# Two-block transformer kernel on one core: zero rows in the latent keys, a written order for the first microseconds, and dilated attention interleaved with the next projections

## The chip, the cores and the metric

The kernel runs on one core of one Trainium2 chip. The metric is the device time of one execution in microseconds (us), taken as the median of the runs.

## The reference

A batch of one with 256 tokens of width 1024 goes through four layers of a first block and one layer of a second block, all in float32. Cut to what matters here:

```python
def mla_attention(x, w_down, q_norm, kv_norm, w_uq, w_ukv, w_o, cos_r, sin_r):   # layer 2 of 4
    ...
    sc = (jnp.einsum('bqhd,bkhd->bhqk', qn_b, k_nope)          # 128 wide, each head its own keys
          + jnp.einsum('bqhd,bkd->bhqk', qr_b, k_rope)) * scale  # 64 wide, one key for all 8 heads
    ...

def swa_sink_attention(x, w_qkv, sinks, w_o, cos, sin):        # layers 0 and 3
    qkv = x @ w_qkv
    ...

def dilated_attention(q, k, v, pos):                           # second block
    # 24 heads of 64 = 3 groups (window 128, 512, 2048; dilation 1, 4, 16) x 8 slots;
    # softmax over the keys of all three groups of a slot, partial rotary on q and k
    ...

def second_block(x, ...):
    proj = rmsnorm(h) @ w_in
    rq, rk, rv, rg, aq, ak, av, gr, ga = jnp.split(proj, ...)
    yr = retention(rq, rk, rv, positions)    # 4 heads
    ya = dilated_attention(aq, ak, av, positions)
    ...
```

## The kernel before

**Arithmetic.** Every projection is done in three passes of a reduced float32 type: each weight and each activation is split into a high part (ACT, line 200) and a low part (DVE, line 201), and TensorE multiplies high by high, high by low and low by high (lines 214 to 216 and 222 to 224, or two wider passes at 248 and 252). The attention products (lines 702, 739, 968, 969, 992, 993, 1234, 1273) use plain float32, and the trace shows two TensorE records for each of them. Transposes go through TensorE with an identity (line 279).

**Data flow.** Weights come from HBM on one queue (SP, line 101) in pieces of 512 KB into five buffers `raw`, and are split into nine pairs of buffers `wh`, `wl`. `Cols.load` issues the DMA and `Cols.get` splits. PSUM has eight banks: `acc` 2, `sc` 2, `tr` 2, `po` 1, `tq` 1. The activation `x` lies as two tiles of 128 tokens, `xT` is its transposed, split form.

**Order.** The program is written as one stream; a scheduler of the tile framework then sets the order on each engine from its own estimate, so that an instruction can pass others on its engine. `Skew.unit` (line 140) runs attention in three steps: the scores and the softmax of a unit, then the transposes of the unit before it (`turn`), then the values of the one before that; `Skew.step` (line 145) takes after these `pieces` steps of a generator `fill`, if one is set. `defer` puts a transpose off until a given number of projection columns has been issued.

**The start.** `setup` (line 379) loads `x[0]` in two halves, two weight pieces of layer 0's key and value projection, `x[1]`, and the other two weight pieces; `x_xT(0)` transposes and splits `x[0]`. `swa` (line 652) then projects keys and values of token tile 0 (`kv(0)`), transposes `x[1]`, does `kv(1)`, the queries, and fills its attention units with `memkv` (line 409): the memory inputs `mem` are loaded into the four buffers `e` and transposed, and projected by `mem_w_kv`.

**Layer 2, latent attention** (`mla`, line 901). `krT` holds the 64-wide rotary key of all heads, transposed, twice: in rows 0 to 63 and 64 to 127. `qrT` holds the rotary queries of two heads in each 128 rows. `scores` (line 963) adds, for each token tile, a product over 128 rows (line 968) and one over 64 rows (line 969), in the upper or lower half of rows by the parity of the head.

**Dilated attention** (`mixer2`, line 1362). For each of four pairs of slots, `dil_proj` (phase dp0 to dp3) projects keys, queries and values of both token tiles (six projections of 24 matmuls) and `dil_attn` (phase da0 to da3) runs two units, one for each token tile. The scores of tile 0 take three groups in two banks `sc`; those of tile 1 take two groups in `sc` and the third in the two banks `acc`, which the projections use too. Two heads lie in the two halves of the rows. After the four pairs comes retention, its first projection in phase rp0.

## Time and profile before

| what | value |
|---|---|
| median of 3 runs | 2066.47 us (2066.15 to 2066.87) |
| the profiled execution's own time | 2067.32 us |
| its span, first to last instruction | 2065.5 us |
| PE busy | 2027.3 us, 98% |
| DVE, ACT busy | 77%, 60% |
| POOL busy | 39.8 us, 2% |
| mean granted TensorE clock | 0.995 |

PE is TensorE's matmul stream and PEld its weight loads; ACT is ScalarE, DVE VectorE, POOL GpSimd, SP the queue that issues the DMAs. A PE record overlaps the next one, so what a matmul costs is read from start to start, not from its duration. In a list of waits, "A <- B" says that A stood idle until B had finished. The granted clock is a share of 2.4 GHz; 0.5 is the lower level of 1.2 GHz.

### The profile page before, as it was taken

The numbers are of one execution on the slowest core, as the hardware profiler recorded it, in microseconds if no ns is written. First come the engines' busy times: TensorE is split into PE (matmuls) and PEld (weight loads), VectorE is DVE, ScalarE is ACT, GpSimd is POOL, SyncE is SP. The second block draws the span as 40 slices with busy tenths as digits, with TensorE's granted clock in tenths as the row PEclk, the third lists the DMA queues.
The fourth block names the chain that finished last, engine by engine and source line by source line (L and its number), as shares of the span: only waits on it lengthen the run. The fifth ranks groups of instructions, "written<-read, shape, count | busy, mean of one in ns | idle before, by whom it ended". The sixth has DMA issues, their size and how long they took to land.

```text
span 2065.5 us, 30420 instructions
## 1 busy us (share of the span) xinstructions
PE 2027.3 (98%) x10741; PEld 1704.8 (83%) x10741; DVE 1587.2 (77%) x3144; ACT 1247.6 (60%) x2592; POOL 39.8 (2%) x54
## 2 busy tenths in 40 slices
PE   7999999999999999999999999999999999999998
PEld 6878888887888888888887788888898888788887
DVE  7766898899699877779888778988666666576666
ACT  5844666595477645557666557665666554456554
POOL 0000000000000000000000000000000000000000
PEclk9999999999999999999999999999999999999999
DMA  7453666446457543555655435764546556566662
GB/s 267 129 166 122 223 204 194 154 135 235 142 179 225 169 161 119 184 189 161 214 163 161 145 127 203 224 191 119 160 120 202 164 175 200 175 193 208 196 187 79
DMA packets 236649, 359.65 MB, mean 174 GB/s; under 512 B 13904, under 2 KB 157392, under 8 KB 236496
## 3 DMA queue, kind: packets, MB, share of 16 engines
q1 hardware_dynamic: 236496, 357.71, 54.8%
q8 instruction: 84, 1.38, 0.3%
q14 instruction: 69, 0.57, 0.1%
HBM read 356.60 MB, written 1.05 MB: 173 GB/s over the span
## 4 chain that ended last, share of the span: by engine, by line
PE 51%; DVE 3%; ACT 2%; issue 1%; DMA 1%; POOL 0%; SPq 0%; POOLq 0%; DVEq 0%; ACTq 0%
PE b2f.sc L248 2%; PE b2f.tr L248 2%; PE b3f.sc L248 1%; PE b3f.tr L248 1%; PE mlp.sc L248 1%; PE mlp.tr L248 1%; PE mlp.acc L214 1%; PE mlp.acc L216 1%; PE mlp.acc L215 1%; PE b2f.acc L216 1%; PE b2f.sc L252 1%; PE b3f.acc L214 1%; PE b2f.acc L214 1%; PE b3f.acc L216 1%; PE b3f.acc L215 1%; PE b2f.acc L215 1%
## 5 line engine op out<-in xcount | busy, mean ns | idle before, releaser
L201 DVE TENSOR_TENSOR mlp.wl<-mlp.raw,mlp.wh 128x512 fp32r<-128x512 f32 x132 | 86.1, 687 | 41.5 <-ACT mlp.wh L200 40.6
L200 ACT ACTIVATE mlp.wh<-mlp.raw 128x512 fp32r<-128x512 f32 x132 | 75.8, 624 | 38.4 <-PE mlp.tq L216 20.8
L200 ACT ACTIVATE b0f.wh<-b0f.raw 128x512 fp32r<-128x512 f32 x132 | 76.3, 623 | 29.7 <-PE b0xo.tq L216 11.1
L200 ACT ACTIVATE b2f.wh<-b2f.raw 128x512 fp32r<-128x512 f32 x132 | 76.2, 623 | 29.1 <-PE b2xo.tq L216 11.0
L200 ACT ACTIVATE b1f.wh<-b1f.raw 128x512 fp32r<-128x512 f32 x132 | 76.2, 622 | 28.6 <-PE b1xo.tq L216 11.2
L200 ACT ACTIVATE b3f.wh<-b3f.raw 128x512 fp32r<-128x512 f32 x132 | 76.4, 622 | 25.9 <-PE b3xo.tq L216 9.8
L201 DVE TENSOR_TENSOR b0f.wl<-b0f.raw,b0f.wh 128x512 fp32r<-128x512 f32 x132 | 85.6, 684 | 5.2 <-ACT b0f.wh L200 5.0
L201 DVE TENSOR_TENSOR b2f.wl<-b2f.raw,b2f.wh 128x512 fp32r<-128x512 f32 x132 | 85.6, 683 | 4.7 <-ACT b2f.wh L200 4.6
L201 DVE TENSOR_TENSOR b1f.wl<-b1f.raw,b1f.wh 128x512 fp32r<-128x512 f32 x132 | 85.6, 684 | 4.6 <-ACT b1f.wh L200 4.4
L201 DVE TENSOR_TENSOR b3f.wl<-b3f.raw,b3f.wh 128x512 fp32r<-128x512 f32 x132 | 85.7, 683 | 4.2 <-ACT b3f.wh L200 3.9
L248 PE MATMUL b3f.sc<-b3xo.xT,b3f.wh 128*128 128x512 f32 x144 | 52.4, 398 | 1.0 <-DVE b3f.e L545 1.0
L248 PE MATMUL b1f.sc<-b1xo.xT,b1f.wh 128*128 128x512 f32 x144 | 52.4, 398 | 0.0
L248 PE MATMUL b2f.sc<-b2xo.xT,b2f.wh 128*128 128x512 f32 x144 | 52.4, 398 | 0.0
L248 PE MATMUL b0f.sc<-b0xo.xT,b0f.wh 128*128 128x512 f32 x144 | 52.4, 398 | 0.0
L248 PE MATMUL b2f.tr<-b2xo.xT,b2f.wh 128*128 128x512 f32 x144 | 51.8, 395 | 0.0
L248 PE MATMUL b0f.tr<-b0xo.xT,b0f.wh 128*128 128x512 f32 x144 | 51.7, 394 | 0.0
L248 PE MATMUL b1f.tr<-b1xo.xT,b1f.wh 128*128 128x512 f32 x144 | 51.7, 394 | 0.0
L248 PE MATMUL b3f.tr<-b3xo.xT,b3f.wh 128*128 128x512 f32 x144 | 51.7, 394 | 0.0
L545 DVE SCALAR_TENSOR_TENSOR b1f.e<-b1f.p,b1x.cols,b1f.e 128x255 f32<-128x255 f32 (+1 forms) x72 | 34.2, 479 | 6.8 <-ACT b1f.e L543 6.3
L545 DVE SCALAR_TENSOR_TENSOR b2f.e<-b2f.p,b2x.cols,b2f.e 128x255 f32<-128x255 f32 (+1 forms) x72 | 34.2, 478 | 6.8 <-ACT b2f.e L543 6.4
L545 DVE SCALAR_TENSOR_TENSOR b0f.e<-b0f.p,b0x.cols,b0f.e 128x255 f32<-128x255 f32 (+1 forms) x72 | 34.2, 478 | 5.7 <-ACT b0f.e L543 5.3
L545 DVE SCALAR_TENSOR_TENSOR b3f.e<-b3f.p,b3x.cols,b3f.e 128x255 f32<-128x255 f32 (+1 forms) x72 | 34.2, 478 | 5.6 <-ACT b3f.e L543 5.1
(1642 smaller groups left out, 7081.5 us busy)
## 6 DMA issues: line engine op xcount, KB each, us to landing
b0f.raw<-in_f_w_up_dram SPq DMA_DIRECT2D x44, 512.0 KB
b1f.raw<-in_f_w_up_dram SPq DMA_DIRECT2D x44, 512.0 KB
b2f.raw<-in_f_w_up_dram SPq DMA_DIRECT2D x44, 512.0 KB
b3f.raw<-in_f_w_up_dram SPq DMA_DIRECT2D x44, 512.0 KB
mlp.raw<-in_w_up_dram SPq DMA_DIRECT2D x32, 512.0 KB
mlp.raw<-in_w_down_dram SPq DMA_DIRECT2D x32, 512.0 KB
b0f.raw<-in_f_w_down_dram SPq DMA_DIRECT2D x22, 512.0 KB
b1f.raw<-in_f_w_down_dram SPq DMA_DIRECT2D x22, 512.0 KB
```

Of the source, the lines that this page charges most:

```text
L200: self.nc.scalar.activation(hi, src, AF.Copy)
L201: self.nc.vector.tensor_sub(lo, src, hi.bitcast(F32))
L214: mm(ps, Th[:, k, tok(t)], wh, start=start, stop=False)
L215: mm(ps, Th[:, k, tok(t)], wl, start=False, stop=False)
L216: mm(ps, Tl[:, k, tok(t)], wh, start=False, stop=stop)
L248: mm(ps.rearrange("p a n -> p (a n)"), wh[:, cs], self.xT[:, k].rearrange("p a n -> p (a n)"), start=k == 0, stop=k == w.K - 1)
L252: mm(ps[:, 1], wl[:, cs], self.xTh[:, k], start=False, stop=False)
L545: nc.vector.scalar_tensor_tensor(hc[:, j, s:], ps[j][:, : T - s], cc[:, 2 - s, f : f + 1], hc[:, j, s:], ALU.mult, ALU.add)
```

## The change

It has three parts that share no instruction.

1. **Start.** Each engine's order is fixed by hand (TensorE, ACT, DVE) from the first instruction to the end of the key and value projection. TensorE begins with 8 transposes of the identity that nobody reads, then those of `x[0]`, then 10 more idle ones; the projections of the two token tiles run interleaved, the second two weight pieces behind, into `acc` and `po`. The first weight piece comes in two DMAs, `x[1]` in two halves between the weights.
2. **Latent keys.** `krT` gets a copy for each parity of the head, the other 64 rows zero (one memset on POOL, and four copies of 64 rows instead of two of 128 on DVE), and the 64-row product becomes one over 128 rows.
3. **Dilated attention.** `dil_proj` becomes a generator of six pieces; three pieces of the next pair's projections (for the last pair: of retention's first) are taken after each unit's scores. In the scores of tile 1 both banks `sc` and both banks `acc` are read before the maxima are taken.

```diff
+WARM = (8, 10)
...
-        for n in range(2):
-            nc.sync.dma_start(self.x[0][:, col(n)], I["x"][0, tok(0), col(n)])
-        for k in (0, 2):
-            self.first.load(k)
-        nc.sync.dma_start(self.x[1], I["x"][0, tok(1), :])
+        rows(0, 0)
+        rows(0, 1)
+        self.first.load(0, True)
+        rows(1, 0)
+        self.first.load(2)
+        rows(1, 1)
         for k in (4, 6):
             self.first.load(k)
...
+    def warm(self, n):
+        ps = self.ps("sc", (4, P))
+        for j in range(n):
+            self.nc.tensor.transpose(ps[:, j % 4], self.ident, self.ident)
...
+        def kv_first():
+            pss = [self.ps("acc"), self.ps("po")]
+            with self.in_order():
+                self.warm(WARM[0])
+                for n in range(2):
+                    self.x_xT(0, n)
+                self.warm(WARM[1])
+                for s in range(KD + 2):
+                    if s < KD:
+                        self.mm_nat(pss[0], self.xTh, self.xTl, s, 0, wkv.get(s), s == 0, s == KD - 1)
+                    if s in (1, 4):
+                        self.x_xT(1, s // 4)
+                    if s >= 2:
+                        self.mm_nat(pss[1], self.xTh, self.xTl, s - 2, 1, wkv.get(s - 2), s == 2, s == KD + 1)
...
-        krT = mp.tile([P, T], F32, name=self.nm("krT"))
+        krT = mp.tile([P, 2, T], F32, name=self.nm("krT"))
+        nc.gpsimd.memset(krT, 0.0)
...
-                    nc.tensor.matmul(o, qrT[r0 : r0 + 64, t, hl // 2], krT[r0 : r0 + 64, :nk], start=False, stop=True)
+                    nc.tensor.matmul(o, qrT[:, t, hl // 2], krT[:, hl % 2, :nk], start=False, stop=True)
...
-        for sp in range(4):
-            self.phase = f"dp{sp}"
-            pr = self.dil_proj(sp)
+        pr, rp = [], []
+        for _ in self.named("dp0", self.dil_proj(pr, 0)):
+            pass
+        sk.pieces = 3
+        for sp in range(4):
+            nx = rp if sp == 3 else []
+            sk.fill = self.named("rp0", self.ret_proj(nx, 0)) if sp == 3 else self.named(f"dp{sp + 1}", self.dil_proj(nx, sp + 1))
             self.phase = f"da{sp}"
             self.dil_attn(sp, pr, *ya, sk)
-        sk.flush()
+            for _ in sk.fill:
+                pass
+            pr = nx
+        sk.rest()
```

**ACT, the first instructions.** `xT` is the split form of `x`, `raw` and `wh` are the weights of the key and value projection. Before:

```order
L200 ACT_TABLE_LOAD
L200 ACTIVATE b0swa.wh_142<-start.raw_90 128x512 x2
L200 ACTIVATE b0swa.wh_154<-start.raw_92 128x512 x2
L200 ACTIVATE start.xT_99<-start.tr_100 128x4x128
L200 ACTIVATE start.xT_99<-start.tr_107 128x4x128
L200 ACTIVATE b0swa.wh_166<-start.raw_95 128x512 x2
L200 ACTIVATE b0swa.wh_178<-start.raw_97 128x512 x2
```

Now:

```order
L205 ACT_TABLE_LOAD
L205 ACTIVATE start.xT_101<-b0swa.tr_142 128x4x128
L205 ACTIVATE start.xT_101<-b0swa.tr_149 128x4x128
L205 ACTIVATE b0swa.wh_167<-start.raw_90 128x512 x2
L205 ACTIVATE start.xT_101<-b0swa.tr_179 128x4x128
L205 ACTIVATE b0swa.wh_186<-start.raw_94 128x512 x2
L205 ACTIVATE b0swa.wh_204<-start.raw_97 128x512 x2
L205 ACTIVATE start.xT_101<-b0swa.tr_213 128x4x128
```

The split of `x[0]` has moved ahead of the first weights; the first split of `x[1]` stands ahead of the second weight piece.

**SP, the loads around the memory inputs.** `mem` is the memory input, `mem_w_kv` its weights. Before:

```order
L101 DMA b0swa.raw_1020<-in_mem_w_kv_dram 128x4x256
L101 DMA b0swa.raw_1040<-in_mem_w_kv_dram 128x4x256
L101 DMA b0swa.raw_1109<-in_mem_w_kv_dram 128x2x512
L101 DMA b0swa.raw_1123<-in_mem_w_kv_dram 128x2x512
L416 DMA b0swa.e_527<-in_mem_dram 128x512
L416 DMA b0swa.e_536<-in_mem_dram 128x512
```

Now:

```order
L106 DMA b0swa.raw_1045<-in_mem_w_kv_dram 128x4x256
L106 DMA b0swa.raw_1065<-in_mem_w_kv_dram 128x4x256
L434 DMA b0swa.e_552<-in_mem_dram 128x512
L434 DMA b0swa.e_561<-in_mem_dram 128x512
L434 DMA b0swa.e_619<-in_mem_dram 128x512
L434 DMA b0swa.e_628<-in_mem_dram 128x512
L106 DMA b0swa.raw_1134<-in_mem_w_kv_dram 128x2x512
```

The memory inputs have moved ahead of two of the ten weight pieces that were issued before them.

**PE, the first pair of dilated attention.** `da0.sc` and `da0.acc` are scores, `dp1.acc` a projection of the next pair, `da0.tr` the transposes of tile 0's probabilities. Before, the end of tile 0's scores and what follows:

```order
L1234 MATMUL da0.sc_14901<-dp0.B_14558,dp0.C_14559 128x128
L1234 MATMUL da0.sc_14902<-dp0.B_14558,dp0.C_14559 128x128
L1234 MATMUL da0.acc_14936<-dp0.B_14558,dp0.C_14559 128x256
L1234 MATMUL da0.acc_14937<-dp0.B_14558,dp0.C_14559 128x256
L1234 MATMUL da0.sc_14926<-dp0.B_14558,dp0.C_14559 128x256 x2
L1234 MATMUL da0.sc_14927<-dp0.B_14558,dp0.C_14559 128x256 x2
L214 MATMUL dp1.acc_14970<-dp1.wh_14975,b3f.xT_14437 128x384
L215 MATMUL dp1.acc_14970<-dp1.wl_14976,b3f.xT_14437 128x384
L216 MATMUL dp1.acc_14970<-dp1.wh_14975,b3f.xT_14437 128x384
```

Now, the scores of tile 1, which stand 72 projection matmuls and two groups of transposes behind those of tile 0:

```order
L1283 MATMUL da0.sc_15143<-dp0.B_14586,dp0.C_14587 128x256
L1283 MATMUL da0.sc_15144<-dp0.B_14586,dp0.C_14587 128x256
L1283 MATMUL da0.sc_15143<-dp0.B_14586,dp0.C_14587 128x256
L1283 MATMUL da0.sc_15144<-dp0.B_14586,dp0.C_14587 128x256
L1283 MATMUL da0.acc_15151<-dp0.B_14586,dp0.C_14587 128x256
L1283 MATMUL da0.acc_15152<-dp0.B_14586,dp0.C_14587 128x256
L284 MATMUL da0.tr_15173<-ident,da0.p_14923 128x128 x3
L284 MATMUL da0.tr_15179<-ident,da0.p_14924 128x128 x3
L284 MATMUL dp1.tq_15206<-ident,dp1.e_15129 128x128 x3
L219 MATMUL dp1.acc_15184<-dp1.wh_15027,b3f.xT_14465 128x384
L220 MATMUL dp1.acc_15184<-dp1.wl_15028,b3f.xT_14465 128x384
```

The two tiles' scores stood next to each other and now stand apart; the projection that needs a bank `acc` again stands behind nine transposes.

## Rows read from the trace of the kernel before

**Rows 1.** The page, part 1: busy us (share of the span) xinstructions.
```profile
PE 2027.3 (98%) x10741; PEld 1704.8 (83%) x10741; DVE 1587.2 (77%) x3144; ACT 1247.6 (60%) x2592; POOL 39.8 (2%) x54
```
**Rows 2.** Timeline of PE, 0 to 20 us: start, us, engine, instruction [idle before].
```profile
3.91 1.94 PE L279 MATMUL start.tr<-ident,x 128*128 128x128 f32 x8 [3.91 <-DMA x<-in_x_dram]
...
10.32 0.79 PE L214 MATMUL b0swa.acc<-b0swa.wh,start.xT 128*128 128x512 f32 x1 [4.46 <-ACT start.xT L200]
...
14.39 0.63 PE L214 MATMUL b0swa.acc<-b0swa.wh,start.xT 128*128 128x512 f32 x1
14.82 0.51 PE L215 MATMUL b0swa.acc<-b0swa.wl,start.xT 128*128 128x512 f32 x1
15.17 0.39 PE L216 MATMUL b0swa.acc<-b0swa.wh,start.xT 128*128 128x512 f32 x1
...
19.81 0.50 PE L214 MATMUL b0swa.acc<-b0swa.wh,start.xT 128*128 128x512 f32 x1 [0.61 <-ACT start.xT L200]
```
**Rows 3.** Timeline of ACT, 3 to 13 us.
```profile
7.25 1.15 ACT L200 ACTIVATE b0swa.wh<-start.raw 128x512 fp32r<-128x512 f32 x2 [5.24 <-DMA start.raw<-in_a_w_qkv_dram]
...
9.69 1.06 ACT L200 ACTIVATE start.xT<-start.tr 128x512 fp32r<-128x512 f32 x2
```
**Rows 4.** Waits of PE, whole span: us in total, times, longest us.
```profile
PE b0swa.tq L279 <- DMA b0swa.e<-in_mem_dram: 1.6, 1, 1.6
```
**Rows 5.** Timeline of the SP queue, 25 to 60 us.
```profile
25.98 19.35 SPq L101 DMA_DIRECT2D b0swa.raw<-in_mem_w_kv_dram  x10
45.39 3.83 SPq L416 DMA_DIRECT2D b0swa.e<-in_mem_dram  x4
```
**Rows 6.** Stretches: us, PE, PEld, DVE, ACT, POOL busy, granted clock, DMA share, GB/s.
```profile
50.00:55.00 5.00, 3.45 (x16) 2.82 (x17) 2.27 (x7) 3.44 (x14) 0.00 (x0) 0.76 0.50 184
1435.00:1440.00 5.00, 4.98 (x22) 4.90 (x23) 2.36 (x8) 2.63 (x5) 0.00 (x0) 0.66 0.27 80
1460.00:1465.00 5.00, 3.27 (x12) 3.19 (x13) 3.47 (x11) 2.90 (x10) 0.00 (x0) 0.73 0.39 111
```
**Rows 7.** Timeline of PE, layer 2: one head's scores and what follows.
```profile
768.98 0.38 PE L968 MATMUL b2mla.sc<-b2mla.q 128*128 128x128 f32 x2
769.29 0.49 PE L969 MATMUL b2mla.sc<-b2mla.krT,b2mla.qrT 64*128 64x128 f32 x2
...
770.96 0.39 PE L222 MATMUL b2mla.acc<-b2mla.cq,b2mla.wh 128*128 128x256 f32 x1
```
**Rows 8.** Timeline of PE, layer 0's cross attention: float32 scores over 128 rows.
```profile
158.99 1.02 PE L462 MATMUL b0x.sc<-memk,b0x.q 128*128 128x256 f32 x4
159.85 0.64 PE L279 MATMUL b0x.tq<-ident,b0x.e 128*128 128x128 f32 x4
```
**Rows 9.** Line 928: duration ns min/median/max, first and last start us.
```profile
L928 DVE COPY b2mla.krT<-b2mla.tr x2: 282/283/284, 764.6 to 764.8; 128x128 f32<-128x128 f32 x2
```
**Rows 10.** Timeline of PE, 1452 to 1472 us: the first pair of dilated attention.
```profile
1453.90 0.33 PE L215 MATMUL dp0.acc<-dp0.wl,b3f.xT 128*128 128x384 f32 x1
1454.07 0.33 PE L216 MATMUL dp0.acc<-dp0.wh,b3f.xT 128*128 128x384 f32 x1
...
1454.86 0.94 PE L1234 MATMUL da0.sc<-dp0.B,dp0.C 64*128 64x128 f32 x12
1455.63 0.60 PE L1234 MATMUL da0.acc<-dp0.B,dp0.C 64*128 64x256 f32 x4
1457.48 1.59 PE L1234 MATMUL da0.sc<-dp0.B,dp0.C 64*128 64x256 f32 x8 [1.25 <-DVE da0.p L1237]
1461.73 0.41 PE L214 MATMUL dp1.acc<-dp1.wh,b3f.xT 128*128 128x384 f32 x1 [2.66 <-DVE da0.pb L1237]
...
1471.88 0.38 PE L279 MATMUL dp1.tq<-ident,dp1.e 128*128 128x128 f32 x2
```
**Rows 11.** Timeline of DVE, second pair: masking of tile 1's scores in `sc`, then `acc`.
```profile
1495.21 1.29 DVE L1237 SCALAR_TENSOR_TENSOR da1.p<-da1.sc,dmask 128x512 f32<-128x512 f32 x2 [0.37 <-PE da1.sc L1234]
...
1497.99 0.75 DVE L1237 SCALAR_TENSOR_TENSOR da1.pb<-da1.acc,dmask 128x256 f32<-128x256 f32 x2
```

More of the change, by code (lines that the diff above doesn't have):

```diff
@@ L89, in __init__, with load @@
         self.got, self.raws = {}, {}
-    def load(self, k):
+    def load(self, k, apart=False):
         net, ncol = self.net, self.ncol
@@ L99, in load @@
             dst = r[:, : n * ncol]
-            if len(src.shape) == 3:
+            if apart:
+                for i in range(n):
+                    net.nc.sync.dma_start(dst[:, i * ncol : (i + 1) * ncol], src[:, i])
+            elif len(src.shape) == 3:
                 net.nc.sync.dma_start(dst.rearrange("p (a n) -> p a n", a=n), src)
@@ L394, in setup, with rows @@
         self.first = self.cols(I["a_w_qkv"][0], 1024, 512)
-        for n in range(2):
-            nc.sync.dma_start(self.x[0][:, col(n)], I["x"][0, tok(0), col(n)])
-        for k in (0, 2):
-            self.first.load(k)
-        nc.sync.dma_start(self.x[1], I["x"][0, tok(1), :])
+        def rows(t, n):
+            nc.sync.dma_start(self.x[t][:, col(n)], I["x"][0, tok(t), col(n)])
+        rows(0, 0)
[4 more added lines that the diff above has]
+        rows(1, 1)
         for k in (4, 6):
@@ L402, in setup, with in_order, x_xT @@
         self.new_xT()
-        self.x_xT(0)
-    def x_xT(self, t):
-        for n in range(2):
-            self.to_xT(t, n, self.x[t][:, col(n)])
+    def in_order(self):
+        E = mybir.EngineType
+        return self.tc.manual_schedule(engines={E.PE, E.Activation, E.DVE})
+    def warm(self, n):
+        ps = self.ps("sc", (4, P))
+        for j in range(n):
+            self.nc.tensor.transpose(ps[:, j % 4], self.ident, self.ident)
+    def x_xT(self, t, n):
+        self.to_xT(t, n, self.x[t][:, col(n)])
     def memkv(self, mp):
@@ L665, in kv, with kv_heads @@
             self.proj_nat(ps, self.xTh, self.xTl, t, wkv)
+            kv_heads(t, ps)
+        def kv_first():
[12 more added lines that the diff above has]
+                        self.mm_nat(pss[1], self.xTh, self.xTl, s - 2, 1, wkv.get(s - 2), s == 2, s == KD + 1)
+            for t in range(NT):
+                kv_heads(t, pss[t])
+        def kv_heads(t, ps):
             nc.scalar.activation(v[:, t], ps[:, 256:512], AF.Copy)
@@ L753, in swa @@
         out = mo(oTh, oTl)
-        kv(0)
         if j:
+            kv(0)
             kv(1)
@@ L768, in swa @@
         else:
-            self.x_xT(1)
-            kv(1)
+            kv_first()
             qT = q(0, 0)
@@ L927, in norm, with turn @@
             self.rope(pb[:, None, 256:320], 1, t, [kd[:, 0:1], kd[:, 1:2]])
-            self.defer(KRW * 512, None, lambda: nc.vector.tensor_copy(
-                krT[:, tok(t)], self.transp(kd.rearrange("p a d -> p (a d)"), 1)[:, 0]))
+            def turn():
+                pt = self.transp(kd.rearrange("p a d -> p (a d)"), 1)[:, 0]
+                for par in range(2):
+                    r = slice(64 * par, 64 * par + 64)
+                    nc.vector.tensor_copy(krT[r, par, tok(t)], pt[r])
+            self.defer(KRW * 512, None, turn)
         sc = 192.0 ** -0.5
@@ L959, in attn @@
             hl = h % 4
-            r0 = 64 * (hl % 2)
             p = self.s("p", [384])
@@ L1166, in o4, with dil_proj @@
         return [self.op.tile([P, 4, T], F32R, tag=t, name=self.nm(t)) for t in ("oh", "ol")]
-    def dil_proj(self, sp):
+    def dil_proj(self, out, sp):
         nc = self.nc
@@ L1176, in dil_proj @@
         kT, qT, v = self.b2("B", [3, T]), self.b2("C", [3, T]), self.b2("A", [2, 384])
+        out += [qT, kT, v]
         wk, wq, wv = cols(7680), cols(6144), cols(9216)
@@ L1198, in dil_proj @@
             roped(wk, kT, t)
+            yield
             roped(wq, qT, t)
+            yield
         for t in range(NT):
@@ L1203, in dil_proj @@
             nc.scalar.activation(v[:, t], ps, AF.Copy)
-        self.need()
-        return qT, kT, v
+            if t:
+                self.need()
+            yield
     def dil_attn(self, sp, qkv, yh, yl, sk):
@@ L1239, in scores @@
                                                        ALU.mult, ALU.add)
-                    if i == 0:
-                        for h in range(2):
-                            nc.vector.tensor_reduce(mx[:, 0, h : h + 1], sms[h][0].rearrange("p g n -> p (g n)"), AX, ALU.max)
-                    else:
-                        nc.vector.tensor_reduce(mx[:, 1], both, AX, ALU.max)
-                        nc.vector.tensor_tensor(mx[:, 0], mx[:, 0], mx[:, 1], ALU.max)
+                for h in range(2):
+                    nc.vector.tensor_reduce(mx[:, 0, h : h + 1], sms[h][0].rearrange("p g n -> p (g n)"), AX, ALU.max)
+                if t:
+                    nc.vector.tensor_reduce(mx[:, 1], both, AX, ALU.max)
+                    nc.vector.tensor_tensor(mx[:, 0], mx[:, 0], mx[:, 1], ALU.max)
                 nc.vector.tensor_scalar_mul(nm, mx[:, 0], -1.0)
@@ L1380, in ret_out @@
                                 lambda a, n=n: a[:, col(n)])
-        self.phase = "rp0"
-        rp = []
-        for _ in self.ret_proj(rp, 0):
-            pass
         sgr, sga = [], []
```

## The prediction

> **What bounds the kernel now.** I read the page's busy shares first. TensorE (PE) is busy for 98% of the span, and no other engine for more than 77% [rows 1]. A part of the change can gain only in two ways: by removing one of the short stretches in which PE waits or runs at the lower clock, or by making PE's own work shorter. The list of waits and the timelines show where each part of the change touches such a stretch. The reader should look in them at the starts of PE's rows, and at the idle time in brackets.
>
> *Start.* PE transposes `x[0]` from 3.91 us and then stands still until 10.32, 4.46 us of it for the split of `xT` on ACT [rows 2]. ACT has done nothing until the first weights landed at 7.25. It then splits two weight pieces, and `xT` only at 9.69 [rows 3]. From 10.32 the projections run at 1.2 GHz: two starts lie 0.43 us apart at 14.39, and the duration of one falls from 0.63 to 0.39 us at 15.17, so the clock rose to 2.4 GHz shortly before [rows 2]. PE waits once more, 0.61 us, for `x[1]` at 19.81 [rows 2]. PE then waits 1.6 us for the memory inputs [rows 4]. Their DMAs stood at 45.39 behind ten weight loads that took the queue 19.35 us [rows 5]. The granted clock of that stretch is 0.76 [rows 6].
>
> *Latent keys.* One head's scores take PE from 768.98 to 770.96, 1.98 us. The switch to the 64-row form shows in the rows: two passes of 128 columns over 128 rows start 0.31 us before the first 64-row pass [rows 7]. Four float32 passes of 256 columns over 128 rows, in another stage, take 158.99 to 159.85 together, 0.215 us each [rows 8].
>
> *Dilated attention.* In the first pair the two tiles' scores stand next to each other, and nothing but the softmax is there to do. PE waits 1.25 and 2.66 us, and the next stretch of 45 projection matmuls ends only at 1471.88 [rows 10], with a granted clock of 0.73 between 1460 and 1465 [rows 6]. I did not find such holes in the other three pairs.
>
> **The change, part by part.** The sum is made against the profiled execution's 2067.32 us; the median of the runs lies 0.85 us lower.
>
> *1, the start.* The 18 idle transposes need no data and stand in PE's holes. At the lower clock a transpose costs 1.94 / 8 = 0.24 us [rows 2], so 8 take 1.9 us, before the data's 3.91, and 10 take 2.4 us, from 5.8 to some 8.2. With `xT` ahead of the weights on ACT, the first projection waits for the first weights alone: they land no earlier than 7.25, since the same bytes stand ahead of them, and one split takes 1.15 / 2 = 0.58 us [rows 3], hence 7.8; the idle transposes could hold it to 8.2. I take 7.8, since a rising clock shortens them; that is 2.5 us before 10.32. If the clock is up by then, the 4.6 us from 10.32 to 14.9 at half speed [rows 2] no longer cost 2.3. The 0.6 us at 19.81 goes too. That is 5.4. Against it stands a new wait: on ACT the second weight piece is now split behind the first half of `x[1]`, whose transposes follow six projections on PE; 1.06 / 2 + 0.58 = 1.1 us [rows 3], and DVE's low parts run beside it. **4.3 us** remain; bounds 2.0 (the clock stays low as long as today) and 5.4.
>
> The memory inputs move ahead of two of ten weight loads on SP, so 19.35 / 10 = 1.9 us each [rows 5] or some 3.9 us earlier, while PE comes there some 4 us earlier. I take it that the 1.6 us [rows 4] go, since the burst of loads ahead of them is shorter, and the clock with them: 0.76 over 5 us is 2.4 us at half speed, 1.2 us [rows 6]. The two loads that they pass hold weights used late in the stage; if this cover fails, PE pays at most the 1.9 us of one load. **2.8 us**, bounds 0 and 2.8.
>
> *2, the latent keys.* With all passes over 128 rows a head needs four of 256 columns at 0.215 [rows 8] and four of 128; half the columns make an estimate of 0.11. The sum is 1.30 us for 1.98, so 0.68 us for each of 8 heads: **5.4 us**. The matmul after the switch may gain another 0.1 each; that is the upper bound, 6.2. The lower bound is nothing, if the softmax of a head sets the pace. I take 5.4: the PE timeline has no hole there today. DVE gets two more copies of 0.28 us [rows 9], before the heads start, beside PE's projections; without that cover they cost 0.6. The memset on POOL, which is busy for 2% [rows 1], is issued a layer earlier.
>
> *3, dilated attention.* From the first scores to 1471.88 takes 17.02 us. The same instructions without waits: scores of tile 0 up to 1455.63, 0.77; of tile 1 at most 0.60 + 1.59; six transposes at half of 0.24, 0.7; 45 projection matmuls at 1454.07 - 1453.90 = 0.17, 7.8 [rows 2, 10]. That makes 11.5, a gain of 5.5: the two waits (3.9), 1.35 us of clock (0.73 over 5 us [rows 6]) and some switching. What covers the softmax then is 72 projection matmuls, 12 us. Where the cover is thin is behind tile 1's scores: the next projection needs a bank `acc`, which DVE frees after masking the two `sc` tiles (1.29) and the two `acc` tiles (0.75) [rows 11]. DVE can begin once the first scores are done, and PE has the rest of the scores and nine transposes to do meanwhile, so I expect under 0.5 us there. The other three pairs lose a split of tile 1's scores around transposes; no row prices that, bounds 0 and 2, and I take 1.0, nearer to the bound that the smooth rows suggest. **6.5 us**, bounds 4.5 (a new wait of 1 us, nothing from the other pairs) and 7.5. The loads of the decay tables on SP move with the units; they are used once a head of retention.
>
> The Trainium skill, "TensorEngine Tiling (Array Packing)", section "Overview", says that a contraction of 64 or less can run up to twice as fast in tiles of 64 rows, because tiles in different rows work independently. It speaks against filling up with zero rows; by it the latent part would lose instead of gaining. The trace decides: in the dilated scores, where both halves hold a head, 12 passes of 128 columns take 0.77 us, 0.064 each [rows 10]; but a head of the latent layer uses one half only, and its 64-row passes have no partner.
>
> Sum: 4.3 + 2.8 + 5.4 + 6.5 = 19.0 us. 2067.32 - 19.0 = 2048.3, and at the median's level 2066.47 - 19.0 = **2047.5 us**.
>
> **The rivals.** What a measurement can tell from no change is about 0.2%, 4.1 us.
>
> *A, the start gives back.* The idle transposes leave the clock where it is, and the memory inputs, the DMAs being no faster than before, are waited for as today. For it: the eight real transposes at 3.91 were followed by projections at 1.2 GHz [rows 2], though 4.5 idle us lie between. Against it: the second batch closes this gap. It costs 2.3 + 2.8 us: 2052.6. The Trainium skill, "TensorE: Matmul & The Clock Gate", section "Part 4: PE-mode transpose", says that the full clock does not engage for transposes; by that rule this rival's first half holds. No row here decides it. I give it 0.16 as a whole.
>
> *B, the zero rows gain nothing.* If the softmax sets the pace of the heads, 5.4 is missing: 2052.9. If 64-row passes in different halves do overlap, as in the dilated scores, the full rows even cost: two passes at 0.11 - 0.064 and two at 0.215 less 1.59 / 8 = 0.20 [rows 8, 10], 0.12 us a head, 1.0 in all, so 2053.9. Against both stands the 1.98 us itself [rows 7], which passes that overlap or wait for nothing can't explain. Together 0.14. The tiling page named above would have the second.
>
> *C, slower: the units fight for banks.* The projections now stand between all scores and share `acc` (and retention's first ones `sc`) with them. If each of the eight units then stops PE as the first pair does today, 2.66 us [rows 10] and 1.35 us of clock [rows 6], they cost 8 x 4.0 = 32 us: 2047.5 + 32 = 2079.5. It outweighs the gains from 19.0 / 8 = 2.4 us a unit on. For it: DVE works in order, and weight splits can stand ahead of the masking. Against it: in the order for the first pair nine transposes stand between, and the first bank needs 2 us. 0.03.
>
> *D, the change doesn't do what it says.* The scheduler already drew ten projection matmuls into the first pair, and what PE saves early it may wait for later, at DMAs. Then the time stays within 0.2%. Against it: the latent part shortens PE's own work. 0.05.
>
> **How the numbers follow.** The forecast gets 0.62, A 0.16, B 0.14, C 0.03, D 0.05. Faster by over 0.2% are the forecast, A and B: 0.92; the same D: 0.05; slower C: 0.03. The range begins where the upper bounds of the parts (1.1 + 0.8 + 1.0) and one dip of the clock elsewhere that moves away, like that at 1435 (0.66 over 5 us, 1.7 us [rows 6]), add up, 4.6 below: 2042.9. It ends 2 us above B's dearer case, room for half of A on top of it: 2056.0.
>
> **What would show it.** Right: PE's first projection near 7.8 us, with starts 0.22 us apart by 9; no wait on the memory inputs and a clock of 1.00 around 50; 1.3 us for a head's scores in layer 2 and no new idle there; no idle over 0.5 us in phases da0 to da3. Wrong: starts 0.43 us apart until 12 or later (A), PE waiting for the softmax in layer 2 (B), waits of `acc` on DVE behind tile 1's scores (C).

## The result, and the profile after

| | before | after |
|---|---|---|
| median of 4 runs, same chip | 2066.31 us (2065.15 to 2066.87) | 2048.61 us (2047.92 to 2050.74) |
| ratio of the times | | 0.9917, 95% interval 0.9906 to 0.9928 |
| the profiled execution: time, span | 2067.32, 2065.5 us | 2047.92, 2046.1 us |
| PE idle in the span (span less busy) | 38.2 us | 27.2 us |

The medians lie 17.7 us apart; 2047.5 us was predicted. Between the two profiled executions it is 19.4 us of span: the one of after is its fastest of four, and the one of before, taken apart from the four timed runs, is slower than all of them. The lines of the page that answer to [rows 1]:

```profile
PE 2018.9 (99%) x10759; PEld 1701.3 (83%) x10759; DVE 1586.5 (78%) x3146; ACT 1244.9 (61%) x2592; POOL 40.2 (2%) x55
```

PE has 18 instructions more, the idle transposes, and is busy for 8.4 us less. Where the time went is read best from the first PE row of each phase in the two timelines:

| PE reaches | before, us | after, us | earlier by |
|---|---|---|---|
| the first scores of layer 0 | 37.78 | 34.78 | 3.0 |
| phase b0mo (layer 0's output projection) | 122.83 | 117.22 | 5.6 |
| phase b2mla (latent attention) | 737.86 | 732.26 | 5.6 |
| phase b2mo | 807.49 | 796.27 | 11.2 |
| phase b3x (last cross attention) | 1169.38 | 1157.92 | 11.5 |
| phase b3xo | 1208.59 | 1196.06 | 12.5 |
| phase dp0 | 1423.15 | 1410.56 | 12.6 |
| phase da0 (dilated scores) | 1454.86 | 1440.83 | 14.0 |
| phase ra0 (retention) | 1616.86 | 1597.56 | 19.3 |
| phase ple (the end) | 2034.31 | 2015.01 | 19.3 |

Five steps stand out: 3.0 and 2.6 at the start, 5.6 in the latent layer, 1.44 between dp0 and da0, 5.3 in the dilated part; 1.06 comes between b3x and b3xo, and some 0.3 in scattered places. Two of these steps, 1.44 and 1.06, lie where the change does nothing.

**Start.** PE's timeline of after, as in [rows 2]; the first six rows are an answer for 0 to 14 us, the others are from one for 6.5 to 48 us, which cuts the second batch of idle transposes at its last six.

```profile
1.36 1.97 PE L422 MATMUL b0swa.sc<-ident 128*128 128x128 f32 x8 [1.36 <-POOL ident masks.py:199]
3.58 2.02 PE L284 MATMUL b0swa.tr<-ident,x 128*128 128x128 f32 x8 [0.26 <-DMA x<-in_x_dram]
5.40 1.71 PE L422 MATMUL b0swa.sc<-ident 128*128 128x128 f32 x10
6.90 0.50 PE L219 MATMUL b0swa.acc<-b0swa.wh,start.xT 128*128 128x512 f32 x1
7.62 0.50 PE L220 MATMUL b0swa.acc<-b0swa.wl,start.xT 128*128 128x512 f32 x1 [0.23 <-DVE b0swa.wl L206]
...
8.67 0.39 PE L221 MATMUL b0swa.acc<-b0swa.wh,start.xT 128*128 128x512 f32 x1
...
6.25 0.86 PE L422 MATMUL b0swa.sc<-ident 128*128 128x128 f32 x6
...
10.71 0.50 PE L219 MATMUL b0swa.acc<-b0swa.wh,start.xT 128*128 128x512 f32 x1 [1.21 <-ACT b0swa.wh L205]
11.51 0.50 PE L220 MATMUL b0swa.acc<-b0swa.wl,start.xT 128*128 128x512 f32 x1 [0.30 <-DVE b0swa.wl L206]
...
25.39 0.66 PE L284 MATMUL b0swa.tq<-ident,b0swa.q 128*128 128x128 f32 x4 [0.40 <-ACT b0swa.kT L709]
...
34.78 1.16 PE L741 MATMUL b0swa.sc<-b0swa.kT,b0swa.q 64*128 64x128 f32 x16 [0.31 <-ACT b0swa.q L716]
```

From start to start the first four idle transposes of the second batch take (6.25 - 5.40) / 4 = 0.21 us each, the last six (6.90 - 6.25) / 6 = 0.11. So the clock rose from 1.2 to 2.4 GHz at about 6.3 us, and PE had executed nothing but transposes until then. The first projection comes at 6.90. The brackets show five waits, 2.45 us together. A pass after a wait takes 0.50 us and not 0.39, and the next start comes later for it. From start to start the five places cost 0.40, 1.46, 0.48, 0.55 and 0.38 us more than the same kinds of passes next to each other without a wait, some 3.3 us together.

The longest, 1.21 us, was foreseen: ACT splits the second tile's first half before the second weight piece.

```profile
6.21 1.29 ACT L205 ACTIVATE b0swa.wh<-start.raw 128x512 fp32r<-128x512 f32 x2
9.54 0.60 ACT L205 ACTIVATE start.xT<-b0swa.tr 128x512 fp32r<-128x512 f32 x1 [2.04 <-PE b0swa.tr L284]
10.03 2.22 ACT L205 ACTIVATE b0swa.wh<-start.raw 128x512 fp32r<-128x512 f32 x4
```

**Memory inputs.** The SP queue has eight loads ahead of them, not ten [rows 5], and no wait on them is left:

```profile
25.92 15.40 SPq L106 DMA_DIRECT2D b0swa.raw<-in_mem_w_kv_dram  x8
41.38 4.82 SPq L434 DMA_DIRECT2D b0swa.e<-in_mem_dram  x4
```

The work of the three stretches of [rows 6] comes some 4, 13 and 14 us earlier now and has the full clock (columns as there; 45 to 50 has 1.00 too). Between the first and the last microseconds one fall of the clock is left, at 460 us (0.66 from 460 to 465); before there were four, at 53, 466, 1435 and 1462.

```profile
50.00:55.00 5.00, 5.00 (x27) 3.58 (x27) 4.36 (x12) 4.36 (x13) 0.00 (x0) 1.00 0.19 73
1423.00:1428.00 5.00, 5.00 (x32) 4.97 (x31) 3.54 (x7) 3.75 (x9) 0.00 (x0) 1.00 0.35 102
1445.00:1450.00 5.00, 5.00 (x32) 4.97 (x31) 1.27 (x7) 2.19 (x6) 0.00 (x0) 1.00 0.50 144
```

**Latent keys.** One head in PE's timeline, as in [rows 7]:

```profile
763.36 0.38 PE L1013 MATMUL b2mla.sc<-b2mla.q 128*128 128x128 f32 x2
763.58 0.39 PE L1014 MATMUL b2mla.sc<-b2mla.krT,b2mla.qrT 128*128 128x128 f32 x2
763.81 0.60 PE L1013 MATMUL b2mla.sc<-b2mla.q 128*128 128x256 f32 x2
764.24 0.59 PE L1014 MATMUL b2mla.sc<-b2mla.krT,b2mla.qrT 128*128 128x256 f32 x2
764.48 0.47 PE L227 MATMUL b2mla.acc<-b2mla.cq,b2mla.wh 128*128 128x256 f32 x1
```

The scores take 1.12 us to the start of the next projection pass, for 1.98 before. Part of that is only moved: the pass after them now takes 0.31 us to the next start and took 0.22. So 0.77 a head here; the whole stage, b2mla to b2mo, fell from 69.63 to 64.01 us, 5.6 or 0.70 a head.

**Dilated attention.** First pair, PE behind the scores of tile 1, to be set against [rows 10], and DVE in the same microseconds:

```profile
1455.09 1.13 PE L1283 MATMUL da0.sc<-dp0.B,dp0.C 64*128 64x256 f32 x8
...
1458.73 0.45 PE L219 MATMUL dp1.acc<-dp1.wh,b3f.xT 128*128 128x384 f32 x1 [0.94 <-DVE da0.pb L1286]
```
```profile
1455.72 0.26 DVE L1232 TENSOR_TENSOR dp1.q<-dp1.e,dC 128x96 f32<-128x96 f32 x1 [0.20 <-ACT dp1.e L1229]
...
1456.46 0.69 DVE L206 TENSOR_TENSOR dp2.wl<-dp2.raw,dp2.wh 128x512 fp32r<-128x512 f32 x1
1457.07 1.28 DVE L1286 SCALAR_TENSOR_TENSOR da0.p<-da0.sc,dmask 128x512 f32<-128x512 f32 x2
1458.26 0.74 DVE L1286 SCALAR_TENSOR_TENSOR da0.pb<-da0.acc,dmask 128x256 f32<-128x256 f32 x2
```

The waits of 1.25 and 2.66 us are gone; one of 0.94 took their place, since DVE rotates a piece of dp1 and splits a weight of dp2 before it begins to mask. The fourth pair has waits of 0.6 us (PE for ACT's copy of transposed probabilities) and 0.4.

### The profile page after: what moved, and what is told of

Its sections match the earlier page's. It is cut to its first block, busy times and chain, and to the rows that moved or that the text cites. A ratio compares the mean times of both kernels' runs of the same rounds, so it can differ in the third digit from the quotient of the medians.

```text
span 2046.1 us, 30433 instructions
## 1 busy us (share of the span) xinstructions
PE 2018.9 (99%) x10759; PEld 1701.3 (83%) x10759; DVE 1586.5 (78%) x3146; ACT 1244.9 (61%) x2592; POOL 40.2 (2%) x55
## 4 chain that ended last, share of the span: by engine, by line
PE 51%; DVE 4%; ACT 2%; issue 1%; DMA 1%; POOL 0%; SPq 0%; DVEq 0%; POOLq 0%; ACTq 0%
PE b2f.sc L253 2%; PE b2f.tr L253 2%; PE b3f.sc L253 1%; PE b3f.tr L253 1%; PE mlp.sc L253 1%; PE mlp.tr L253 1%; PE mlp.acc L219 1%; PE mlp.acc L221 1%; PE mlp.acc L220 1%; PE b3f.acc L219 1%; PE b3f.acc L220 1%; PE b3f.acc L221 1%; PE b2f.acc L221 1%; PE b2f.sc L257 1%; PE b2f.acc L219 1%; PE b2f.acc L220 1%
```

## The experiments

The kernel before was run beside each group. On these chips its own times scatter more than in the first comparison (2063.69 to 2074.42 us in 21 runs of the first group), so medians with their intervals tell the sign, and the length of one stretch in the trace tells the size. The intervals of the variants of the changed kernel overlap its own, and three of them ran once, so there the traces alone carry the reading. "Local" below is such a stretch, between the first PE rows of two phases of the same profile.

**Each part alone**, on the kernel before. The zero rows:

```diff
-        krT = mp.tile([P, T], F32, name=self.nm("krT"))
+        krT = mp.tile([P, 2, T], F32, name=self.nm("krT"))
+        nc.gpsimd.memset(krT, 0.0)
...
-                    nc.tensor.matmul(o, qrT[r0 : r0 + 64, t, hl // 2], krT[r0 : r0 + 64, :nk], start=False, stop=True)
+                    nc.tensor.matmul(o, qrT[:, t, hl // 2], krT[:, hl % 2, :nk], start=False, stop=True)
```

> The kernel before with the padded key tile of the latent layer alone. My theory (a pass over 64 rows costs nothing extra by itself, but each change between 128 and 64 rows holds PE up): one head's scores fall from 1.98 us to about 1.3, phase b2mo begins 5.5 us earlier, and the time is 5.5 us (0.27%) below before's. Rival (the softmax paces the heads, or the gain is eaten by a wait of the next head): the scores get shorter but b2mo begins less than 2 us earlier. Rival (passes of 64 rows were overlapping): b2mo begins up to 1 us later.

Measured: 2062.37 us for 2068.12, ratio 0.9976 (0.9966 to 0.9986). Locally b2mla to b2mo takes 63.92 us, 5.7 less than before. The theory holds, both rivals fall. b2mo itself is only 2.7 us earlier, because this execution had lost 3.0 us ahead of the layer, 2.7 of them by b0mo: PE waited 2.5 us and not 1.6 for the memory inputs, and the low clock behind it lasted longer (0.53 from 52 to 57 us).

The start (of its edit only the calls are shown; the rest is as in the change):

```diff
-        kv(0)
         if j:
+            kv(0)
...
-            self.x_xT(1)
-            kv(1)
+            kv_first()
```

> The kernel before with the start of the change alone (load order, order of the first microseconds, idle transposes, both tiles' first projections side by side). My theory from the two traces: the first scores of layer 0 begin 3.0 us earlier and phase b0mo 5.6 us earlier, of which 2.6 are the wait for the memory inputs and the dip of the clock that follows it; the rest of the program is unmoved, so the time is 5.6 us below before's. Rival (what was saved early is waited for later): b0mo 5.6 us earlier, but less than 3 us at the end. Rival (the memory inputs' gain came from another part of the change): b0mo only 3 us earlier.

Measured: 2061.05 us, ratio 0.9972 (0.9959 to 0.9984), 7.1 us less. The first scores come at 34.95 us, 2.8 earlier, b0mo 5.4 earlier. Nothing was given back: the end is 7.8 us earlier, because two dips of the clock went as well, 0.6 us of it by b1xo and 1.8 between dp0 and da0. The second is the fall at 1435 of [rows 6], in work which this kernel's edit does not touch and which lies some 6 us earlier here:

```profile
1430.00:1435.00 5.00, 5.00 (x30) 5.00 (x30) 3.52 (x10) 4.30 (x10) 0.00 (x0) 1.00 0.44 127
```

The dilated part:

```diff
+        for _ in self.named("dp0", self.dil_proj(pr, 0)):
+            pass
+        sk.pieces = 3
         for sp in range(4):
...
+            sk.fill = self.named("rp0", self.ret_proj(nx, 0)) if sp == 3 else self.named(f"dp{sp + 1}", self.dil_proj(nx, sp + 1))
```

> The kernel before with the dilated part alone (next group's projections in pieces, later maxima). My theory: phases da0 to the start of retention shorter by 5.3 us, nearly all of it in the first pair, and the time 5.3 us below before's; the dip of the clock at the beginning of da0, which is missing in the changed kernel, belongs to the position in time and not to this part, so it stays here or comes back elsewhere (then 5.3 less 1.5 to 1.7). Rival (the dip goes with the maxima's order or the new order of the units): 6.7 us, with a granted clock of 1.00 from 1430 to 1470.

Measured: 2062.54 us, ratio 0.9971 (0.996 to 0.9982), 5.6 us less. Locally da0 to ra0 takes 156.8 us for 162.0, 5.2 less; 4.6 of it in the first pair (da0 to da1). The dip at 1435 is missing here too (1.8 us between dp0 and da0), though the waits ahead of it are as before (1.0 and 0.7 us), and another came between b3x and b3xo. It is present with the zero rows alone and with the next run's edit, neither of which reaches the place. And it is back, some 1 us between dp0 and da0, in three of the changed kernel's variants below (later transposes, and either batch alone), whose edits do not reach the place either. So no part of the change decides over it; what makes it come and go stays open.

**What the 64-row passes cost.**

```diff
-                    nc.tensor.matmul(o, qk[:, 0, tok(t)], qk[:, 1, :nk], start=True, stop=False)
-                    nc.tensor.matmul(o, qrT[r0 : r0 + 64, t, hl // 2], krT[r0 : r0 + 64, :nk], start=False, stop=True)
+                    u = qk[:, 0, tok(t)], qk[:, 1, :nk]
+                    w = qrT[r0 : r0 + 64, t, hl // 2], krT[r0 : r0 + 64, :nk]
+                    for i, ab in enumerate((w, u) if t else (u, w)):
+                        nc.tensor.matmul(o, *ab, start=i == 0, stop=i == 1)
```

> The kernel before, without zero rows; of each head's four score products of the latent layer the last two stand in the other order, so that the row form changes twice per head and not four times; the sums are the same. Theory (each change of the form costs): 4 changes cost the 0.70 us per head that the change gained, so two of them 0.35, 2.8 us over 8 heads, b2mo 2.8 us earlier. Rival (the 64-row passes are slow in themselves, whatever stands next to them): nothing, within 0.3 us in b2mo.

Measured: 2064.31 us, ratio 0.9982 (0.9973 to 0.999). Locally b2mla to b2mo takes 66.66 us, 2.97 less than before: half of the change's gain for half of the changes of form, with the same passes. One head on PE:

```profile
769.25 0.38 PE L971 MATMUL b2mla.sc<-b2mla.q 128*128 128x128 f32 x2
769.56 0.92 PE L971 MATMUL b2mla.sc<-b2mla.krT,b2mla.qrT 64*128 64x128 f32 x4
770.41 0.70 PE L971 MATMUL b2mla.sc<-b2mla.q 128*128 128x256 f32 x2
770.76 0.47 PE L222 MATMUL b2mla.acc<-b2mla.cq,b2mla.wh 128*128 128x256 f32 x1
771.06 0.28 PE L223 MATMUL b2mla.acc<-b2mla.cq,b2mla.wh 128*128 128x256 f32 x1
```

From the first score pass to the second projection pass it is 2.20 us with four changes of form (768.98 to 771.18 before), 1.81 here with two, 1.43 with none: 0.19 us for each change. The 64-row passes are not slow in themselves. The Trainium skill, "TensorEngine Tiling (Array Packing)", section "Key Properties", says that changing the tiling mode drains TensorE; the three runs agree that a change costs time, and price it for this kernel; a drain itself is not seen in the rows.

**The idle transposes**, left out of the changed kernel altogether, then one batch at a time (what they write is read by nobody):

```diff
-WARM = (8, 10)
+WARM = (0, 0)
```

> The changed kernel without the 18 idle transposes; all else as it is. In the changed kernel the clock was up by 6.9 us, and PE had done nothing but transposes until then. Theory (the idle transposes lifted it): the first projections run at 0.43 us each instead of 0.23, the clock rises only some microseconds after 6.9, and the first scores of layer 0 come 1 to 2.3 us later; the mechanism of the memory inputs is untouched. Rival (transposes never count, the clock would have risen at the same time anyway, or the stage waits for weights): starts 0.23 apart from the first projection on, and the first scores within 0.3 us of the changed kernel's.

Measured: 2052.09 us, ratio 0.9922 (0.9907 to 0.9936). The first scores come at 37.28 us, 2.5 later than with them. On PE the first projection starts no later, but at half speed, and full speed comes only at 15.3:

```profile
6.85 0.80 PE L219 MATMUL b0swa.acc<-b0swa.wh,start.xT 128*128 128x512 f32 x1 [1.20 <-ACT b0swa.wh L205]
...
8.25 0.63 PE L221 MATMUL b0swa.acc<-b0swa.wh,start.xT 128*128 128x512 f32 x1
...
15.32 0.48 PE L219 MATMUL b0swa.acc<-b0swa.wh,start.xT 128*128 128x512 f32 x1
15.64 0.40 PE L220 MATMUL b0swa.acc<-b0swa.wl,start.xT 128*128 128x512 f32 x1
```

The theory holds. Stated in the other direction, the idle transposes are worth 2.5 of the start's 3.0 us; earlier weights and order alone gain 0.5. The changed kernel's profile is the best of six with this start, though: the first scores come between 34.78 and 36.22 us in them, so the transposes are worth 1.1 to 2.5.

With WARM = (8, 0) and (0, 10):

> The changed kernel with the first batch of 8 idle transposes alone; the 10 behind the first tile's transposes are left out. Theory of the prediction (the second batch closes the gap in which PE would stand still before the projections, so the clock needs it): the projections begin at 1.2 GHz, starts 0.43 us apart, and the first scores of layer 0 come at about 37, as without any idle transposes (37.28). Rival (the sum of PE's work counts, not the gap): 8 idle and 8 real transposes are enough, starts 0.23 apart from the first projection on and the first scores near 34.8.

> The changed kernel with the second batch of 10 idle transposes alone; the 8 before the first tile's data are left out. Theory: PE then works without a hole from its first real transpose at about 3.7 us on, and the clock rises about 2.3 us later than in the changed kernel (where PE began at 1.36 and was up at the first full-speed row, 6.3 us): some five projections at half speed, the first scores about 1 us later than 34.78. Rival (the first batch does nothing): within 0.3 us.

Measured, one run each: 2054.68 and 2051.67 us. With the first batch alone the projections run at half speed (starts 0.43 us apart to 9.99) and the first scores come at 37.44: the second batch is the one that counts, as its theory said. The 37.44 holds a second loss, however: starts were 0.23 us apart by 13.3, and at 14.1 the granted clock fell again. With the second alone the first scores come at 35.31. That is 0.5 us later than in the changed kernel's profile, between theory (1) and rival (0.3). But in five other profiles with both batches they come between 34.9 and 36.2, so whether the first batch does anything stays open.

**The second tile's transposes later**, so that ACT splits the second weight piece first:

```diff
-                for s in range(KD + 2):
...
+                for c, k in ("A0", "A1", "A2", "X0", "A3", "B0", "B1", "X1", "A4", "B2", "A5", "B3",
+                             "A6", "B4", "A7", "B5", "B6", "B7"):
```

(A and B are the projections of the two tiles, X the transposes of the second, the number is the weight slice or the half.)

> The changed kernel with the second tile's transposes later among the first projections: the second weight piece is split on ACT ahead of the second tile's first half, not behind it. Theory (the 1.21 us wait for that split and the 0.30 behind it are what the order of ACT costs): these waits go, the first scores of layer 0 begin 1.2 to 1.5 us earlier than 34.78, and the time falls by as much. Rival (weights arrive no faster): the projections run earlier by 1 us or more at 12 us, but the next stage waits for its weights' DMAs, and the first scores gain less than 0.4 us.

Measured: 2052.37 us, ratio 0.9924 (0.9909 to 0.9938), not distinguishable from the changed kernel's 0.9917. On PE the piece comes 1.37 us earlier, the first scores 0.49:

```profile
9.34 0.50 PE L219 MATMUL b0swa.acc<-b0swa.wh,start.xT 128*128 128x512 f32 x1 [0.42 <-ACT b0swa.wh L205]
...
34.29 1.16 PE L743 MATMUL b0swa.sc<-b0swa.kT,b0swa.q 64*128 64x128 f32 x16
```

and b0mo 0.5 later than in the changed kernel. The wait is real, but two thirds of it are taken back before the first scores: between 11.5 and 13.0 us passes start 0.34 to 0.39 us apart where the changed kernel has 0.23, and by 16 us only 0.46 is left. The rival's number, under 0.4, was slightly too low, and its mechanism is not shown: from 16 to 34 us ACT waits less for weights' DMAs here (1.3 us) than in the changed kernel (2.4). The rest goes between the first scores and b0mo, without a longer wait: the 192 passes of 256 columns of the memory projections take 24.7 us from start to start and not 23.7, with passes of the attention between them in more places.

**The place of the maxima**, back where it was:

```diff
-                for h in range(2):
-                    nc.vector.tensor_reduce(mx[:, 0, h : h + 1], sms[h][0].rearrange("p g n -> p (g n)"), AX, ALU.max)
-                if t:
-                    nc.vector.tensor_reduce(mx[:, 1], both, AX, ALU.max)
-                    nc.vector.tensor_tensor(mx[:, 0], mx[:, 0], mx[:, 1], ALU.max)
+                    if i == 0:
+                        for h in range(2):
+                            nc.vector.tensor_reduce(mx[:, 0, h : h + 1], sms[h][0].rearrange("p g n -> p (g n)"), AX, ALU.max)
+                    else:
...
```

> The changed kernel with the maxima back where they stood, between the masking of the two sc banks and that of the two acc banks. Theory (DVE's order decides when an acc bank is free for the next projection): the first bank is freed two reduces later, 1.27 us, so PE's wait behind tile 1's scores in the first pair grows from 0.94 to about 2, and up to 1.27 us come in each of the other three pairs: phases da0 to ra0 1.2 to 5 us longer, most likely 2.5, with one more dip of the clock possible (1.7 us). Rival (the units between the scores do all of it, the maxima's place is worth nothing): within 0.4 us.

Measured: 2055.09 us, ratio 0.9933 (0.9918 to 0.9948). Locally da0 to ra0 takes 158.96 us for 156.73, 2.2 more. The size is as expected, the place is not: PE's waits in the list are spread over three pairs, and the first pair's did not grow.

```profile
PE dp2.acc L219 <- DVE da1.pb L1286: 1.0, 1, 1.0
PE dp3.acc L219 <- DVE da2.pb L1286: 1.0, 1, 1.0
PE dp1.acc L219 <- DVE da0.pb L1286: 0.8, 1, 0.8
```

In this kernel's order on PE the scheduler has put five score products of the next pair (ten records, 1.31 us) into the first pair's gap. The bank itself comes free later, as the theory had it: from tile 1's scores to the next projection it is 4.83 us and not 3.64. Put back, the maxima cost 2.2 of the 5.2 us, and with them in their old place the interleaving still gains 3.0; as PE's order moved too, this is no clean division between the two.

**The acc banks masked first**, then with the positions' DMA early:

```diff
+                for i, gs in reversed(list(enumerate(parts))):
                     for h in range(2):
-                        nc.vector.scalar_tensor_tensor(sms[h][i], pss[h], 0.125,
+                        nc.vector.scalar_tensor_tensor(sms[h][i], psl[i][h], 0.125,
```

> The changed kernel with DVE masking the acc banks before the sc banks in the second tile's scores (as scheduled, between the two sc banks). Theory (the wait of 0.94 us in the first pair is the bank's): the first acc bank is free 0.64 us earlier and phases da0 to ra0 shrink by about 0.6. Rival (another wait is behind it): nothing, or a longer wait elsewhere in da0 to da3.

Measured: 2050.27 us, ratio 0.9914 (0.9897 to 0.993). Locally da0 to ra0 takes 156.44 us, 0.3 less; the wait fell from 0.94 to 0.7. Right in direction, half the size; the next run, with the same masking, shows 0.7 again, and four more profiles without it 0.94 or 0.95.

```diff
-        pb = self.s("e", [T], I32)
+        self.cos = self.cp.tile([P, NA], F32, name="cos")
+        pb = self.cos[:, :T].bitcast(I32)
```

> The changed kernel with two further edits: the masking order of the acc banks as in the run before, and the positions' DMA into a tile of its own (the later cosine tile), so that it is issued a layer earlier and DVE no longer waits for it in the last cross attention (0.8 us in the changed kernel's profile, 1.8 to 2.0 in five other profiles; PE waits 1.0 and 2.0 to 2.2 us behind it). Theory: phase b3x to b3xo takes 38.1 us or less down to 37.1 (38.1 in the changed kernel's profile, 39.2 to 41 in the others), da0 to ra0 0.3 us less, in all 1.3 to 2.5 us below the changed kernel. Rival (another wait of DVE is behind it): b3x to b3xo still 38.5 or more.

Measured: 2047.93 us (2047.19 to 2048.37), ratio 0.9903 (0.9887 to 0.992), the lowest median of the study. Locally b3x to b3xo takes 37.28 us, and PE has no wait left in it; da0 to ra0 takes 156.32, 0.4 less. These are 1.3 us less than in the changed kernel's profile, but the intervals of the two ratios overlap: a better version by its trace, not shown faster by its times.

**Less cover between the two tiles' scores:**

```diff
-        sk.pieces = 3
+        sk.pieces = 2
```

> The changed kernel with two pieces of the next group's projections behind each tile's scores instead of three; the last two pieces follow behind the pair. So 48 projection matmuls, 8.3 us, stand between the two tiles' scores and not 72, 12.5 us. Theory of the prediction (the cover is longer than the softmax needs): phases da0 to ra0 within 0.5 us. Rival (the softmax of a tile needs most of the 12.5 us, because DVE and ACT split weights in between): PE waits 1 us or more in front of the transposes of the softmax in each pair, 3 to 8 us in all.

Measured, one run: 2056.08 us. Locally da0 to ra0 takes 162.5 us, 5.8 more than in the changed kernel, the old kernel's length again. The first two pairs behave as the theory had it, with waits of 0.6 us or less. The third does not:

```profile
1514.57 0.66 PE L284 MATMUL da2.tr<-ident,da1.pb 128*128 128x128 f32 x4 [3.85 <-ACT da2.pT L1312]
```
```profile
1512.93 0.94 ACT L205 ACTIVATE dp3.wh<-dp3.raw 128x512 fp32r<-128x512 f32 x2 [1.93 <-DVE da2.mx L1290]
...
1513.93 1.07 ACT L1312 ACTIVATE da2.pT<-da2.tr 128x512 f32<-128x512 f32 x2
```
```profile
1515.00:1520.00 5.00, 5.00 (x23) 5.00 (x21) 0.94 (x4) 2.18 (x6) 0.00 (x0) 0.66 0.80 236
```

ACT stood at a weight split of the next pair, which itself waited for DVE, while PE needed the softmax's copy behind it; the granted clock in the next 5 us is 0.66. The last pair waits 1.2 us more, for a bank `sc` in front of retention's projections. So the rival was right in sum and wrong in its pattern: by this trace it is the order of ACT's queue in one place, not the length of the softmax in all of them; no run changes that order alone.

## Why the prediction was right

The time, the sign and the range came out. Term by term the agreement is looser than the sum.

- **Start, 4.3; measured 3.0** (2.8 with this part alone; 1.6 to 3.0 over the six profiles with this start, so 3.0 is luck in part). The first projection came at 6.9 and not 7.8: "they land no earlier than 7.25" was wrong, for ACT splits the first weights at 6.21. They now come in two DMAs, and ACT's first split reads only the first. The clock was up, as taken; the experiment without idle transposes shows that these are worth 2.5 us, in the place of the 2.3 that the prediction gave the clock. What failed is the sentence on the new wait, 1.1 us: that one measured 1.21, but four more around it were not seen, and together the five cost some 3.3 us from start to start. 4.3 + 0.9 - (3.3 - 1.1) = 3.0. The wait of 1.2 us belongs to the new order: it stands in the run without idle transposes too. The waits of 0.23, 0.30 and 0.40 are missing there (the last one, 0.31, is 0.7): these are splits and copies of DVE and ACT that faster projections run into. As the later transposes show, removing the first wait alone brings a third of it.
- **Memory inputs, 2.8; measured 2.6.** No wait, clock 1.00 at 50 us. The dip was read over 50 to 55 us and ran on (0.90 from 55 to 60), so it cost 1.7 us and not 1.2; of the 3.3 that wait and dip then make, 0.7 were not gained, and where they went is not shown. It is not the hour: in the run without idle transposes PE comes there 2.5 us later and the inputs are issued 2.5 us later (43.87), and still no wait comes. All ten profiles with the new start lack the wait, all four with the old one have it (1.6 to 2.5 us). That the place behind fewer loads is the cause is likely and not isolated: in the run with the later transposes nine loads stand ahead and not eight, and no run moves the inputs alone. The 2.6 is the low end: with the old start the stretch from the first scores to b0mo takes 85.1 to 87.8 us in four profiles, and 82.4 in the changed kernel.
- **Latent keys, 5.4; measured 5.6** (5.7 alone). The estimate for a head's scores, 1.30 us, was 1.12 with 0.09 of it moved to the next pass. The prediction put the loss on the switch of the row form; half the switches gave half the gain.
- **Dilated attention, 6.5; measured 5.3** (5.2 alone). The first pair gave 4.6 for 5.5. The step that failed is "I expect under 0.5 us there" for the bank `acc`: it is 0.94, with DVE taking a rotation and a weight split of the projections first; "no idle over 0.5 us in phases da0 to da3" failed there and, with 0.6, in the fourth pair. That is rival C's mechanism at a small price. The other pairs gave 0.7 for 1.0.
- **Not in the sum, 2.5.** The dip at 1435 us is gone, 1.44 us; the range's lower end named it as possible. It goes and stays in the other runs whatever their edit, so it isn't the doing of a part. And 1.06 us between b3x and b3xo comes from a wait that the change leaves in its place: DVE waits for the positions' DMA in the last cross attention, and PE behind it. Before:

```profile
PE b3x.po L490 <- DVE b3x.oTl L201: 2.1, 1, 2.1
DVE ang.q L1122 <- DMA ang.e<-in_positions_dram: 1.8, 1, 1.8
```

and after:

```profile
PE b3x.po L508 <- DVE b3x.oTl L206: 1.0, 1, 1.0
DVE ang.q L1167 <- DMA ang.e<-in_positions_dram: 0.8, 1, 0.8
```

The seven variants of the changed kernel that leave this DMA where it is show 1.8 to 2.0 us for it: the 0.8 is this execution's luck. The parts that the change owns are 3.0 + 2.6 + 5.6 + 5.3 = 16.5 us, for 19.0 in the sum. Some of the agreement is thus chance.

**The rivals.** A needed the idle transposes to do nothing and the memory wait to stay; both fell. The Trainium skill, "TensorE: Matmul & The Clock Gate", section "Part 4: PE-mode transpose", by which the full clock does not engage for transposes, is not borne out here: six transposes at 0.11 us each before any other matmul. The profile writes them as MATMUL and does not tell whether they use the transpose mode that the section is about. B fell with the local 5.7 us and with the halved switches, which gave half the gain with the same 64-row passes. C did not happen, but it is near: one wait of 3.85 us with the clock that follows appeared as soon as two pieces stood where three had. D fell.

## What to carry to other kernels

When a stretch at the lower clock is removed from in front of a stage, price the stage again with every engine at its new distance: some of the copies and splits that the slow passes covered become waits, and each costs more than its bracket. Passes of 64 rows between passes of 128 cost at the changes of form (0.19 us each here), so put them next to each other, or fill up with zeros when only one half is used. A gain that a profile shows in a stretch which the change does not touch (a dip, a late DMA) should be looked up in several profiles before it is credited to the change.

## What the runs showed of the hardware

- Transposes alone brought the clock up, but not at a fixed time. In five of the six profiles with the same start the spacing of the idle transposes falls from 0.21 to 0.11 us between 5.9 and 7.3 us. In the sixth (masking order and positions' DMA) all of them, and the first two projections behind them, still ran at half speed; the second starts 0.42 us before the third:

```profile
5.70 2.34 PE L422 MATMUL b0swa.sc<-ident 128*128 128x128 f32 x10
...
8.27 0.60 PE L220 MATMUL b0swa.acc<-b0swa.wl,start.xT 128*128 128x512 f32 x1
8.69 0.40 PE L221 MATMUL b0swa.acc<-b0swa.wh,start.xT 128*128 128x512 f32 x1
```

- The latest first scores of the six, 36.22 us with the old maxima, have another cause: a granted clock of 0.66 again between 12 and 17 us, behind the waits at 9 to 11.5. The other five have the same waits and no such fall:

```profile
12.00:17.00 5.00, 5.00 (x19) 3.96 (x18) 1.33 (x3) 0.29 (x1) 0.00 (x0) 0.66 1.06 381
```

- The clock column cannot be trusted for the first microseconds. In the changed kernel it says 1.00 while the first eight transposes take 1.97 / 8 = 0.25 us each, over twice the 0.11 of the last six; durations of like passes are the safer reading there:

```profile
1.36:3.30 1.94, 1.94 (x8) 1.56 (x8) 0.00 (x0) 0.65 (x1) 0.00 (x0) 1.00 0.70 230
```
